# Scattering PEER gates with an accumulating DMA instead of overwriting running sums

## Chip, cores and metric

The kernel runs on one core of a Trainium2 chip. The metric is the device time of one execution in microseconds (us); several executions are timed and their median is compared. TensorE (PE), VectorE (DVE), ScalarE (ACT) and GpSimd (POOL) are the computing engines of the core, and SyncE (SP) only issues DMAs here. POOL issues DMAs too, by an instruction of its own for each (in the profile: DMA_INDIRECT).

## What is computed

One layer of a streaming encoder: a token mixer (two kinds of attention, 8 heads each, one input and one output projection) and then a PEER mixer, in which each token picks single-neuron experts. Only the second half bears on this change. For 512 tokens, 8 PEER heads and 16 experts per head, the reference does this for each block of 128 tokens:

```python
idx = jnp.take_along_axis(cand_i, best_j, axis=-1)       # 8 heads x 16 experts of 16384
g = jax.nn.softmax(best_s, axis=-1)                      # a gate for each
a = gelu(einsum('thkd,td->thk', u_sel, hb))              # u_sel, v_sel: the rows of u and v at idx
out = einsum('thk,thkd->td', g * a, v_sel)
```

The 16 experts of one head are distinct. Two heads of one token can pick the same expert, and then its two gates add up.

## The kernel before, in words

The first 128 tokens are done by gathering: for each of the 128 slots of a token (8 heads by 16) an indirect DMA from POOL (`fetch`, line 824) brings the chosen row of `u`, and later that of `v`, of all 128 tokens into one of three buffers `gr`, 1 MB at a time, and DVE works on it in two halves (`consume`, lines 843 and 846). There are 256 such gathers. `consume(n)` issues the gather of `n + 2`; a buffer comes free when DVE has used the row set that lies in it.

The other 384 tokens (three blocks) are done densely, over all 16384 experts. PE works through a list of items (line 937): A items and D items multiply 128 rows of `u` with the tokens (48 matmuls each, `mm_u`, line 994), R items load activations made earlier, V items multiply by `v` (`mm_v`, line 1016). The list has 108 A items, then 16 D items, then the V and R items. The activation of an A item goes to a DRAM scratch table (`act_out`, line 876). The gates of the dense tokens stand in another DRAM table, `g_scr`, with one number for each expert and token (25 MB), which was zeroed early in the kernel (line 607). D and R items load 192 KB of it (`load_gates`, line 959) and multiply. The first of these loads is issued three items ahead of the first D item.

The table is filled by scatters from POOL: one indirect DMA writes 128 numbers of 4 bytes (one slot of one block of 128 tokens), 8 heads x 16 slots x 3 blocks = 384 of them. A generator, `scatter()` (line 910), hands the work out in steps, and the item loop (line 1049) takes `NSC` steps per A or D item from the third item on (line 1068), with some two of the gathers' halves (`due`, line 858), spread over the four cuts in which the next item's weights are split into a high and a low part (`cut_up`, line 975, with ACT's cast at line 183 and DVE's subtraction at line 184).

Before the change a step of `scatter()` does two things. `total(h, b, i)` (line 911) has DVE compare the expert of one slot with those of all slots of the token up to the same head, and sum the gates where they agree, into `tot`. Then the scatter of the slot of the head before (48 steps earlier) is traced, which writes that sum. An expert that several heads chose is written by each of them in turn, and the last write holds the whole sum. Scatters of one head are declared independent of each other; those of the next head wait until all of the head before have landed. There are 9 x 48 = 432 steps, six per item, so 72 items.

How the order on the engines comes about: inside the item loop PE, DVE, ACT and SP keep the order in which the program is traced (`fixed`, line 1045). POOL is not in that set. Its order is made at build time by a scheduler, which gives POOL the earliest traced instruction among those whose inputs and buffers are ready by its own reckoning; on the chip POOL then works through that order, one after the other.

Of the kernel before, what the change touches and what calls it, by code (L numbers as in the profile page):

```python
# [9 lines left out]
F32 = mybir.dt.float32  # L10
# [5 lines left out]
OP = mybir.AluOpType  # L16
AX = mybir.AxisListType
PSUM = bass.MemoryType.PSUM
DRAM = bass.MemoryType.DRAM

P = 128
# [3 lines left out]
D = 2048  # L25
# [3 lines left out]
TOPK = 16  # L29
PH = 8  # L30
TD0 = 128
TD = T - TD0
NDB = TD // P
# [5 lines left out]
WA = 2.1  # L39
JC = 16  # L40
LEAD = JC // 2 + 1
NSC = 6
AHEAD = 3


class Lanes:
    """Steps of generators, run between pieces of the tensor engine's main stream.

    A generator yields (pieces to wait, next step uses the shared bank)."""

    def __init__(self):
        self.q = {}
# [39 lines left out]
def hymba_peer(ctx: ExitStack, tc: tile.TileContext, xT, w_in, w_fl, b_fg, g_mix, g_q, g_k, g_merge,  # L92
               w_out, g_ffn, w_q, keysT, uT, u, v, out):
    nc = tc.nc

    def pool(name, bufs=1, **kw):
        return tc.tile_pool(name=name, bufs=bufs, **kw)
# [11 lines left out]

    nc.scalar.preload_act_table_set("natural_log_exp_and_others")  # L110

# [1 line left out]
    ident = cst.tile([P, P], F32, name="ident")  # L113
    make_identity(nc, ident)
    identb = cst.tile([P, P], BF16, name="identb")
# [101 lines left out]
    with ExitStack() as fctx:  # L217
        rawx = ExitStack()
        raw = rawx.enter_context(pool("raw", 16))

# [1 line left out]
        KV = [(0, 264), (264, 528)]  # L222
        QR = [(NM, S)]
        raws = [None] * 16

# [1 line left out]
        with ExitStack() as actx:  # L227
            at = actx.enter_context(pool("at", 2))
            qk = actx.enter_context(pool("qk", 1))
# [1 line left out]
            def t2(shape, dtype, name):  # L231
                return at.tile(shape, dtype, name=name, tag="t2", bufs=15)

            # the input, scaled by the gain; each projection is scaled by rstd as it leaves PSUM
            hh, hl = [], []
            flr = raw.tile([P, KD, NH], F32, name="flr", tag="raw")
            flh = raw.tile([P, KD, NH], F32R, name="flh", tag="raw")
# [2 lines left out]
            rstd = raw.tile([P, S], F32, name="rstd", tag="rstd", bufs=1)  # L240
# [3 lines left out]
            for k in range(KD):  # L244
# [25 lines left out]
                a = big.tile([P, S], F32R, name=f"hh{k}", tag="hh")  # L270
                b = big.tile([P, S], F32R, name=f"hl{k}", tag="hl")
# [17 lines left out]
            stx.close()  # L289
            mnx.enter_context(tc.manual_schedule(engines=ordered))  # L290

            # forget gate: cumulative log sigmoid, [head, token]
            fb_ = raw.tile([NH, S], F32, name="fb", tag="raw")
            for i, (lo, hi) in enumerate(KV):
                nc.vector.tensor_tensor(fb_[:, lo:hi], fps[i][:NH, :264], rstd[:NH, lo:hi], op=OP.mult)
# [55 lines left out]
            def pass3(ah, al, bh, bl):  # L351
                return ((ah, bh), (ah, bl), (al, bh))

            # -- stick-breaking head, keys on partitions --
            # (rows, width, [(key block, column offset, first query)])
            units = [(P, 512, [(2, 0, 256), (3, 256, 256)]), (P, 384, [(1, 0, 128)]),
                     (P, 512, [(0, 0, 0)]), (NM, 512, [(4, 0, 0)])]

            def sb_att(c, q, vh, vl):
                zs, sps, tops, sums, wts = {}, {}, {}, {}, {}  # L360
# [25 lines left out]
                    sps[ui] = [(sh, sl, off, t0) for b, off, t0 in blks]  # L386
                    tops[ui] = a

                # sums over the key blocks so far, for the units before them
                def run_on(ui):  # L390
                    a, w = tops[ui], units[ui][1]
                    if ui == 0:
                        w = 256
                        nc.vector.tensor_tensor(a[:, :w], a[:, :w], a[:, w:], op=OP.add)
                    else:
                        pw = sums[ui - 1][2]
                        nc.vector.tensor_tensor(a[:, w - pw:w], a[:, w - pw:w], tops[ui - 1][:, :pw], op=OP.add)
                    rh = t2([P, 512], F32R, f"rh{c}_{ui}")
                    rl = t2([P, 512], F32R, f"rl{c}_{ui}")
                    split(rh[:, :w], rl[:, :w], a[:, :w])  # L400
                    sums[ui] = rh, rl, w
# [74 lines left out]
                lanes.add("misc", v_natural(c, ps, vh, vl), 1, True)  # L476
                lanes.add("att", sb_att(c, q, vh, vl), 1)

            # -- forgetting head, queries on partitions --
            def fox_norm(h, nm, ps, rng, gn, q):  # L480
                off = rng[0][0]
                xs = []
                for i, (lo, hi) in enumerate(rng):
                    w = hi - lo
                    x = t2([P, 512], F32, f"x{nm}{h}{i}")
                    nc.vector.tensor_tensor(x[:, :w], ps[i][:, :w], rstd[:, lo:hi], op=OP.mult)
                    sq = t2([P, 512], F32, f"xs{nm}{h}{i}")
                    nc.scalar.activation(sq[:, :w], x[:, :w], AF.Square)
                    sh = t2([P, 512], F32R, f"xh{nm}{h}{i}")
                    sl = t2([P, 512], F32R, f"xl{nm}{h}{i}")  # L490
                    split(sh[:, :w], sl[:, :w], sq[:, :w])
                    xs.append((x, sh, sl))

                def g():
                    for i, (lo, hi) in enumerate(rng):
                        w = hi - lo
                        x = xs[i][0]
                        pm = pmisc(f"pn{nm}{h}{i}")
                        for n in (1, 2):
                            nc.tensor.matmul(pm[:, :w], nones, xs[i][n][:, :w], start=(n == 1), stop=(n == 2))  # L500
                        y = rsqrt(t2, pm[:, :w], -P, [P, w], f"{nm}{h}{i}")
                        nc.vector.scalar_tensor_tensor(x[:, :w], x[:, :w], gn, y, op0=OP.mult, op1=OP.mult)
                        split(q[nm + "h"][:, lo - off:hi - off], q[nm + "l"][:, lo - off:hi - off], x[:, :w])
                        if i + 1 < len(rng):
                            yield 1, True
                return g()
# [113 lines left out]
            lanes.drain()  # L620
        fcx.close()

# [1 line left out]
        pr = ctx.enter_context(pool("pr", 1, side="right"))  # L624
        hbn = pr.tile([P, D], F32, name="hbn")
        acc = pr.tile([P, D], F32, name="acc")
# [5 lines left out]
        with ExitStack() as mctx:  # L632
# [21 lines left out]
            for _ in merge(1):  # L654
                pass

# [1 line left out]
            ss2 = mt.tile([P, T], F32, name="ss2", bufs=1)  # L658

            def residual(c, ps):  # L660
# [32 lines left out]
            first = [project(w_out[c], mh, ml, [(0, T)], f"wo{c}", hfs=(0,)) for c in range(3)]  # L693
# [6 lines left out]
            ssf = big.tile([P, T], F32, name="ssf", tag="ssf", bufs=1)  # L700
            nc.gpsimd.tensor_copy(ssf, ss2)

# [1 line left out]
        rawx.close()  # L704
        hbx = ExitStack()
        hbd = hbx.enter_context(pool("hbd", 1, side="right"))
# [5 lines left out]
        with ExitStack() as qctx:  # L712
# [89 lines left out]
            for h in range(PH):  # L802
                scs = []
                for p in range(2):
                    c = 2 * h + p
                    key = qp.tile([P, P], F32, name=f"key{c}", tag="key")
# [9 lines left out]

    bigx.close()

# [1 line left out]
    # (table, slot), the up rows of a head before its down rows  # L820
    order = [(x, h * TOPK + i) for h in range(PH) for x in range(2) for i in range(TOPK)]
    rows = {}

# [38 lines left out]
        done[0] = r.stop  # L862
        return [x for n in r for x in (consume(n),) * 2]

# [1 line left out]
    dn = ctx.enter_context(pool("dn", 2))  # L866
    gp = hbx.enter_context(pool("gp", 1, side="right"))
    ef = gp.tile([P, NTB, P], F32, name="ef")
    dst = gp.tile([P, NDB, P], I32, name="dst")
    tot = gp.tile([P, NDB, P], F32, name="tot")  # L870
    def act_out(j, ps, keep=False):
        g = dn.tile([P, TD], F32, name=f"ga{j}", tag="ga")
        nc.scalar.activation(g, ps[:, :TD], AF.Gelu)
# [29 lines left out]
    gt = ctx.enter_context(pool("gt", 3))  # L903
    pq = ctx.enter_context(pool("pq", 2))

    # the gates of the dense tokens, scattered head by head: an expert that several heads chose gets the
    # sum of its gates, written by each of them in turn with the heads so far
    g_flat = g_scr.rearrange("j i (t o) -> (j i t) o", o=1)

    def scatter():  # L910
        def total(h, b, i):
            s, w = h * TOPK + i, (h + 1) * TOPK
            junk = gp.tile([P, P], F32, name=f"junk{h}{b}{i}", tag="junk")
            nc.vector.scalar_tensor_tensor(junk[:, :w], ef[:, b + 1, :w], ef[:, b + 1, s:s + 1],
                                           gts[:, b + 1, :w], op0=OP.is_equal, op1=OP.mult,
                                           accum_out=tot[:, b, s:s + 1])

        slots = [(b, i) for b in range(NDB) for i in range(TOPK)]
        for h in range(PH + 1):
            head = []  # L920
            for b, i in slots:
                if h < PH:
                    total(h, b, i)
                if h > 0:
                    s = (h - 1) * TOPK + i
                    w = nc.gpsimd.indirect_dma_start(  # L926
                        out=g_flat, out_offset=bass.IndirectOffsetOnAxis(ap=dst[:, b, s:s + 1], axis=0),
                        in_=tot[:, b, s:s + 1], in_offset=None)
                    for x in head:
                        tc.declare_no_dep(w.ins, x.ins, reason="the experts of one head differ")  # L930
                    head.append(w)
                yield

    # the tensor engine's order: A(j) makes the activations of experts i*P+j for all i, for later; D(j)
    # makes those of the first chunk, gated at once; R(j) fetches those made before and gates them;
    # V(j, half) adds their values to one half of the output's columns
    items = [("A", j) for j in range(JC + NAP, P)] + [("D", j) for j in range(JC)]
    for c in range(P // JC):
        for x in range(2 * JC):
            half, jj = divmod(x, JC)  # L940
# [7 lines left out]
    def kind(t):  # L948
        return items[t][0] if 0 <= t < len(items) else ""
# [96 lines left out]
    with tc.manual_schedule(engines=fixed):  # L1046
        sc = scatter()
        loaded = 0
        for t in range(len(items) + 1):
# [5 lines left out]
            turn = prev[0] == "V" and prev[1] % JC == JC - 1  # L1055
# [9 lines left out]
            if t == GATES:  # L1065
                gts = gates()
            work = []
            if kind(t) in ("A", "D") and t > GATES:
                work = due(WA) + [sc] * NSC
            elif kind(t) == "V":  # L1070
# [6 lines left out]
            if kind(t) == "V" and items[t][2] == 0 and items[t][1] in (4, 8, 12):  # L1077
                b = len(accd)
# [61 lines left out]
```

## Time and profile before

| | before |
|---|---|
| median of 3 runs | 3520.58 us |
| lowest, highest | 3518.69, 3529.51 us |
| profiled execution, first to last instruction | 3525.9 us |
| mean granted TensorE clock in it | 0.977 of full speed |
| busy: PE, DVE, ACT, POOL | 3398.5, 2402.1, 1296.8, 1096.4 us |

The profile is of one execution. Its time is given as the span from the first to the last instruction, 3525.9 us; no other time of that execution is recorded. The A items lie between 1278 and 2342 us of the span, the D items up to 2477, the V items behind them. Times within the profile are microseconds from the start of the span. A row of the view that groups instructions gives the line, engine, operation, what is written and read, the count, the busy time with the mean of one in ns, and the idle time of the engine just before them with what ended it; "issue" stands for time in which the engine waited for nothing that the profile shows.

### The profile page before, as it was taken

To read this page: it belongs to the slowest core of one execution; us is meant where nothing else is said; L and a number is where in the kernel's file an instruction comes from. 1 tells how busy PE (TensorE), PEld (TensorE's weight loads), DVE (VectorE), ACT (ScalarE), POOL (GpSimd) and SP (SyncE) were. 2 spreads that over 40 slices of the span, in tenths; PEclk is the share of its full clock that TensorE was granted. 3 is DMA by queue.
4 is the path that set the end of the run, shared out by engine and by line. 5 is a ranking of instruction groups with operands and counts; after the bars stand their busy time and mean duration, and the time that the engine had idled before them with its cause. 6 is when DMAs were issued, how large, how long until landed. Compare 5 with 4: busy or idle time off the path is not lost.

```text
span 3525.9 us, 49445 instructions
## 1 busy us (share of the span) xinstructions
PE 3398.5 (96%) x17838; PEld 2999.8 (85%) x17838; DVE 2402.1 (68%) x4939; ACT 1296.8 (37%) x2427; POOL 1096.4 (31%) x916
## 2 busy tenths in 40 slices
PE   8999999999999979789888999999999999999999
PEld 6888899988888779779877899999888888888887
DVE  7555666658449996556656666667777877877775
ACT  5444555444333323222222233333333333333332
POOL 2000000012238637767777611111122122112110
PEclk9999999999999989899888999999999999999999
DMA  3333333323442247667666777888888888888885
GB/s 122 126 105 106 107 106 104 107 87 110 141 132 91 89 147 241 219 204 250 220 205 217 246 287 285 288 292 287 319 305 314 300 313 311 308 310 312 312 306 169
DMA packets 224534, 749.23 MB, mean 212 GB/s; under 512 B 35360, under 2 KB 90784, under 8 KB 190880
## 3 DMA queue, kind: packets, MB, share of 16 engines
q1 hardware_dynamic: 168736, 452.23, 39.4%
q0 software_dynamic: 55552, 293.84, 23.0%
q8 instruction: 140, 2.29, 0.3%
q14 instruction: 106, 0.87, 0.1%
HBM read 690.19 MB, written 55.77 MB: 212 GB/s over the span
## 4 chain that ended last, share of the span: by engine, by line
PE 86%; DVE 8%; issue 3%; DMA 2%; POOL 0%; ACT 0%; SPq 0%; DVEq 0%; POOLq 0%; ACTq 0%
PE pv L1016 30%; PE pa L994 28%; PE pj_wo L212 5%; PE pj_sv L212 3%; PE pj_fv L212 3%; PE pj_sk L212 3%; PE pj_fk L212 3%; PE pj_fq L212 3%; PE pj_fg L212 3%; PE pj_sq L212 2%; DMA gr<-in_u_dram,idx 1%; DVE oh L783 1%; PE pj_wq L212 1%; DVE oh L779 1%; PE po L580 1%
## 5 line engine op out<-in xcount | busy, mean ns | idle before, releaser
L994 PE MATMUL pa<-dh,wl_A 128*128 128x384 f32 x1728 | 599.1, 347 | 46.9 <-DVE wl_A L184 23.3
L994 PE MATMUL pa<-dh,wh_A 128*128 128x384 f32 x1728 | 597.7, 346 | 25.9 <-issue 25.4
L994 PE MATMUL pa<-dl,wh_A 128*128 128x384 f32 x1728 | 598.1, 346 | 22.6 <-issue 22.1
L1016 PE MATMUL pv<-wh_V,pl 128*128 128x512 f32 x1536 | 597.5, 389 | 0.0
L1016 PE MATMUL pv<-wl_V,ph 128*128 128x512 f32 x1536 | 597.5, 389 | 0.0
L1016 PE MATMUL pv<-wh_V,ph 128*128 128x512 f32 x1536 | 597.5, 389 | 0.0
L184 DVE TENSOR_TENSOR wl_A<-wr_u,wh_A 128x512 fp32r<-128x512 f32 x428 | 294.4, 691 | 341.0 <-ACT wh_A L183 218.4
L183 ACT CAST wh_A<-wr_u 128x512 fp32r<-128x512 f32 x432 | 265.5, 620 | 656.2 <-PE pa L994 467.9
L183 ACT CAST wh_V<-wr_v 128x512 fp32r<-128x512 f32 x512 | 317.2, 621 | 507.1 <-PE pv L1016 504.8
L184 DVE TENSOR_TENSOR wl_V<-wr_v,wh_V 128x512 fp32r<-128x512 f32 x510 | 343.2, 689 | 221.7 <-ACT wh_V L183 221.5
L926 POOL DMA_INDIRECT g_scr<-tot,dst x384 | 429.3, 1118 | 149.5 <-issue 84.1
L994 PEld LDWEIGHTS pa<-dh,wl_A 128*128 128x128 f32 x1728 | 335.3, 194 | 61.2 <-issue 35.2
L828 POOL DMA_INDIRECT gr<-in_v_dram,idx x128 | 179.8, 1405 | 631.9 <-DVE acc L846 505.0
L994 PEld LDWEIGHTS pa<-dh,wh_A 128*128 128x128 f32 x1728 | 335.0, 194 | 37.3 <-issue 36.8
L994 PEld LDWEIGHTS pa<-dl,wh_A 128*128 128x128 f32 x1728 | 334.9, 194 | 36.2 <-issue 36.0
L828 POOL DMA_INDIRECT gr<-in_u_dram,idx x128 | 156.6, 1224 | 621.8 <-DVE gr L843 479.7
L1016 PEld LDWEIGHTS pv<-wh_V,ph 128*128 128x128 f32 x1536 | 288.3, 188 | 59.9
L1016 PEld LDWEIGHTS pv<-wl_V,ph 128*128 128x128 f32 x1536 | 288.3, 188 | 59.9
L1016 PEld LDWEIGHTS pv<-wh_V,pl 128*128 128x128 f32 x1536 | 288.3, 188 | 59.8
L843 DVE SCALAR_TENSOR_TENSOR gr<-gr,hbn 128x1024 f32<-128x1024 f32 x256 | 303.0, 1220 | 35.8 <-DMA gr<-in_u_dram,idx 31.1
L846 DVE SCALAR_TENSOR_TENSOR acc<-gr,coef,acc 128x1024 f32<-128x1024 f32 x256 | 318.1, 1284 | 2.0 <-DMA gr<-in_v_dram,idx 1.4
L348 POOL TENSOR_TENSOR osq<-o 128x512 f32<-128x512 f32 x14 | 14.5, 1036 | 525.6 <-ACT o L342 525.6
(388 smaller groups left out, 6197.0 us busy)
## 6 DMA issues: line engine op xcount, KB each, us to landing
wr_u<-in_uT_dram SPq DMA_DIRECT2D x256, 512.0 KB
wr_v<-in_v_dram SPq DMA_DIRECT2D x256, 512.0 KB
g_scr<-zero POOLq DMA_DIRECT2D x16, 1536.0 KB
gg<-g_scr SPq DMA_DIRECT2D x128, 192.0 KB
a_scr<-ga SPq DMA_DIRECT2D x112, 192.0 KB
gb<-a_scr SPq DMA_DIRECT2D x112, 192.0 KB
wr_wo<-in_w_out_dram SPq DMA_DIRECT2D x32, 512.0 KB
wr_wq<-in_w_q_dram SPq DMA_DIRECT2D x32, 512.0 KB
```

The costliest lines, as they stand in the source:

```text
L183: nc.scalar.copy(hi, src)
L184: (lo_eng or nc.vector).tensor_tensor(lo, src, hi.bitcast(F32), op=OP.subtract)
L212: nc.tensor.matmul(ps[i][:, :hi - lo], wt[:, kk, :], ht[k][:, lo:hi], start=(k == 0 and n == 0), stop=(k == KD - 1 and n == 2))
L580: nc.tensor.matmul(po[:, t0:], vv, ww, start=f, stop=True, skip_group_check=not f)
L779: nc.vector.tensor_tensor(oh, abf[:, p].unsqueeze(2).to_broadcast([P, NTB * TOPK, TOPK]), iota16.unsqueeze(1).to_broadcast([P, NTB * TOPK, ...
L783: nc.vector.tensor_tensor(ohv, ohv, i1f[:, :, p, :].unsqueeze(2).to_broadcast([P, NTB, TOPK, TOPK]), op=OP.mult)
L828: nc.gpsimd.indirect_dma_start(out=r, out_offset=None, in_=(u, v)[x], in_offset=bass.IndirectOffsetOnAxis(ap=idx0[:, s:s + 1], axis=0))
L843: nc.vector.scalar_tensor_tensor(r[:, c], r[:, c], 1.0, hbn[:, c], op0=OP.mult, op1=OP.mult, accum_out=dots[:, y, h, i:i + 1])
L846: nc.vector.scalar_tensor_tensor(acc[:, c], r[:, c], coef[:, h, i:i + 1], acc[:, c], op0=OP.mult, op1=OP.add)
L926: w = nc.gpsimd.indirect_dma_start(out=g_flat, out_offset=bass.IndirectOffsetOnAxis(ap=dst[:, b, s:s + 1], axis=0), in_=tot[:, b, s:s + 1] ...
L994: nc.tensor.matmul(ps[:, :TD], wt[:, k % 4, :], ht[k], start=(k == 0 and n == 0), stop=(k == KD - 1 and n == 2))
L1016: nc.tensor.matmul(po["now"][n][b], a[:, bs], w_, start=(jj == 0 and pi == 0), stop=(jj == JC - 1 and pi == 2))
```

## The change

The sums are no longer made. Each of the 384 scatters takes its numbers from the gates themselves (`gts`, the result of `gates()` at line 878) and adds them to what stands in the table (`compute_op=OP.add`). A step is one scatter; four steps are taken per item. The tile `tot` goes, and the loop over slots now has the slot outside and the token block inside. The comments, which the change also strips, are left out here.

```diff
-NSC = 6
+NSC = 4
...
-    tot = gp.tile([P, NDB, P], F32, name="tot")
...
     def scatter():
-        def total(h, b, i):
-            s, w = h * TOPK + i, (h + 1) * TOPK
-            junk = gp.tile([P, P], F32, name=f"junk{h}{b}{i}", tag="junk")
-            nc.vector.scalar_tensor_tensor(junk[:, :w], ef[:, b + 1, :w], ef[:, b + 1, s:s + 1],
-                                           gts[:, b + 1, :w], op0=OP.is_equal, op1=OP.mult,
-                                           accum_out=tot[:, b, s:s + 1])
-
-        slots = [(b, i) for b in range(NDB) for i in range(TOPK)]
-        for h in range(PH + 1):
+        for h in range(PH):
             head = []
-            for b, i in slots:
-                if h < PH:
-                    total(h, b, i)
-                if h > 0:
-                    s = (h - 1) * TOPK + i
+            for i in range(TOPK):
+                for b in range(NDB):
+                    s = h * TOPK + i
                     w = nc.gpsimd.indirect_dma_start(
                         out=g_flat, out_offset=bass.IndirectOffsetOnAxis(ap=dst[:, b, s:s + 1], axis=0),
-                        in_=tot[:, b, s:s + 1], in_offset=None)
+                        in_=gts[:, b + 1, s:s + 1], in_offset=None, compute_op=OP.add)
                     for x in head:
                         tc.declare_no_dep(w.ins, x.ins, reason="the experts of one head differ")
                     head.append(w)
-                yield
+                    yield
```

## Rows read from the trace of the kernel before

**Rows 1.** The page: span, busy time by engine (its part 1), chain by engine (part 4).

```profile
span 3525.9 us, 49445 instructions
...
PE 3398.5 (96%) x17838; PEld 2999.8 (85%) x17838; DVE 2402.1 (68%) x4939; ACT 1296.8 (37%) x2427; POOL 1096.4 (31%) x916
...
PE 86%; DVE 8%; issue 3%; DMA 2%; POOL 0%; ACT 0%; SPq 0%; DVEq 0%; POOLq 0%; ACTq 0%
```

**Rows 2.** Busy time by windows, items A: with scatters, after them, a dense piece.

```profile
core 0: us, PE busy (x) PEld busy (x) DVE busy (x) ACT busy (x) POOL busy (x), PEclk, DMA share, GB/s
1316.00:2036.00 720.00, 638.62 (x3295) 600.02 (x3293) 448.83 (x1273) 195.61 (x345) 514.89 (x457) 0.91 0.70 227
2036.00:2342.00 306.00, 305.46 (x1762) 305.14 (x1761) 193.87 (x280) 105.53 (x186) 49.28 (x41) 1.00 0.81 287
...
2100.00:2200.00 100.00, 100.00 (x579) 100.00 (x578) 63.18 (x75) 34.55 (x60) 17.25 (x14) 1.00 0.80 287
```

**Rows 3.** The same view, four neighbouring stretches while scatters run.

```profile
1573.00:1656.00 83.00, 83.00 (x470) 83.00 (x469) 66.23 (x190) 27.61 (x48) 64.80 (x55) 1.00 0.78 256
1656.00:1700.00 44.00, 29.10 (x97) 20.92 (x96) 13.48 (x41) 6.24 (x11) 30.18 (x30) 0.69 0.47 155
1700.00:1778.00 78.00, 78.00 (x451) 78.00 (x451) 63.73 (x189) 25.86 (x46) 61.41 (x52) 1.00 0.81 261
1778.00:1814.00 36.00, 20.29 (x61) 13.30 (x60) 8.59 (x24) 4.13 (x8) 24.38 (x24) 0.65 0.51 166
```

**Rows 4.** Groups of POOL's instructions, 1316 to 2036 us.

```profile
L926 POOL DMA_INDIRECT g_scr<-tot,dst x384 | 429.3, 1118 | 149.5 <-issue 84.1 <-DVE junk L914 37.3 <-DVE wl_A L184 17.9
L828 POOL DMA_INDIRECT gr<-in_u_dram,idx x41 | 50.4, 1229 | 35.6 <-DVE gr L843 17.3 <-issue 8.8 <-DMA gr<-in_u_dram,idx 8.3
L828 POOL DMA_INDIRECT gr<-in_v_dram,idx x32 | 35.2, 1100 | 15.1 <-issue 7.9 <-DVE acc L846 5.9 <-DVE junk L914 0.6
```

**Rows 5.** POOL in order of time, two gathers with the scatters between them.

```profile
1713.28 0.98 POOL L828 DMA_INDIRECT gr<-in_u_dram,idx  x1 [0.30 <-DMA g_scr<-tot,dst]
1714.57 1.63 POOL L926 DMA_INDIRECT g_scr<-tot,dst  x1 [0.30 <-DVE wl_A L184]
1716.50 1.45 POOL L926 DMA_INDIRECT g_scr<-tot,dst  x1 [0.30 <-DVE gr L843]
1718.26 0.97 POOL L926 DMA_INDIRECT g_scr<-tot,dst  x1 [0.30 <-issue]
1719.53 0.97 POOL L926 DMA_INDIRECT g_scr<-tot,dst  x1 [0.30 <-issue]
1720.81 0.97 POOL L926 DMA_INDIRECT g_scr<-tot,dst  x1 [0.30 <-DVE wl_A L184]
1722.08 1.29 POOL L926 DMA_INDIRECT g_scr<-tot,dst  x1 [0.30 <-DMA g_scr<-tot,dst]
1723.68 1.99 POOL L828 DMA_INDIRECT gr<-in_u_dram,idx  x1 [0.30 <-issue]
```

**Rows 6.** Groups by line, 1316 to 1384.2 us: scatters issued and sums made.

```profile
L926 POOL DMA_INDIRECT g_scr<-tot,dst x38 | 45.9, 1208 | 11.6 <-issue 7.6 <-DVE junk L914 1.5 <-DVE wl_A L184 1.2
...
L914 DVE SCALAR_TENSOR_TENSOR junk<-ef,e 128x16 f32<-128x16 f32 (+1 forms) x49 | 11.4, 232 | 0.9
```

**Rows 7.** DVE's groups of the sums, 1316 to 2036 us.

```profile
L914 DVE SCALAR_TENSOR_TENSOR junk<-ef,e 128x16 f32<-128x16 f32 (+7 forms) x384 | 112.4, 293 | 6.8
...
L914 DVE DVE_READ_ACCUMULATOR junk<-ef,e 128x1 f32 x384 | 31.5, 82 | 0.0
```

**Rows 8.** The scatters' line alone: ns min/median/max, first and last start.

```profile
L926 POOL DMA_INDIRECT g_scr<-tot,dst x384: 963/972/2021, 1318.0 to 2004.7; - x192
L926 POOLq EVENT_SEMAPHORE  x375: 17/17/5282, 1316.3 to 1995.9; - x188
```

**Rows 9.** POOL's groups behind the scatters, 2036 to 2342 us.

```profile
L828 POOL DMA_INDIRECT gr<-in_v_dram,idx x21 | 25.9, 1234 | 132.4 <-DVE acc L846 89.3 <-DVE gr L843 28.7 <-DVE coef L851 14.4
L828 POOL DMA_INDIRECT gr<-in_u_dram,idx x20 | 23.4, 1168 | 135.0 <-DVE gr L843 113.5 <-DVE acc L846 21.5
```

**Rows 10.** The line that loads gates: first and last start.

```profile
L959 SPq DMA_DIRECT2D gg<-g_scr x128: 326/431/1490, 2319.7 to 3421.9; - x128
```

## Prediction

> **What bounds the kernel now.** I read the page first. PE is busy 96% of the span and holds 86% of the chain that ended last [rows 1], so a change on POOL and DVE can only pay where PE is held up. The view by windows shows where. Behind the scatters PE does 579 matmuls in 100 us [rows 2]; at 48 matmuls an item that is 8.29 us an item, the dense pace. While scatters run (1316 to 2036 us) it does 3295, or 68.6 items, in 720 us; at the dense pace these would take 569 us. So **151 us** of the span are lost in this stage, and that is the most the change can gain by speeding it up; the stretch behind it (1762 matmuls in 306 us) loses next to nothing.
>
> Cut finer, the stage falls into two kinds of stretch that alternate [rows 3] (nine thin ones in all; these are two of them). In the dense ones PE is always busy and its clock is granted at 1.00, the level of 2.4 GHz. In the thin ones it does 97 matmuls in 44 us, 61 in 36 us. There the mean grant is 0.69 and 0.65, so part of the time at the lower level of 1.2 GHz, after PE had been left with gaps; that is a consequence. DVE is less busy in the thin stretches than in the dense ones (13.5 of 44 us against 66.2 of 83), so DVE's work is not what is short. The engine that never rests in either is POOL: 64.8 of 83 us, 30.2 of 44 us, and this leaves out 0.30 us in front of nearly every DMA that it issues [rows 5].
>
> That makes POOL's ledger the one to draw up [rows 4]. A scatter costs (429.3 + 84.1) / 384 = 1.337 us of POOL, its "issue" gaps counted. A gather costs (50.4 + 35.2 + 8.8 + 7.9) / 73 = 1.40 us, and there are 73 in 68.6 items, 1.064 an item. At six scatters an item POOL needs 6 x 1.337 + 1.064 x 1.40 = 9.51 us for an item that PE could do in 8.29. **POOL is overloaded while scatters run**, the gathers queue behind scatters on it, and DVE, which works in order, waits for gathers. Behind the scatters POOL waits for DVE instead [rows 9].
>
> **What the change removes.** The 384 sums cost DVE 112.4 + 31.5 = 144 us [rows 7]. DVE is busy 449 of 720 us there [rows 2], under PE's time, so I cost this at nothing on the path; what covers it is DVE's own slack of 271 us. The sums also hold POOL: it waited 37.3 + 17.9 = 55 us for them [rows 4], and these waits go.
>
> **What it adds.** The number of scatters stays 384, with the same 128 offsets and 128 numbers of 4 bytes each. Each must now also read the table. The trace of before has no accumulating DMA. Its bounds are the shortest scatter, 0.963 us, and the longest, 2.021 us [rows 8]; a gain cannot be excluded, since the mean of 1.118 contains scatters stretched beside DVE work that now goes. Of the rows between, the nearest is the gather from `u`, 1.229 us [rows 4], which also issues 128 reads of HBM at offsets. I take it: 0.111 us more for each, 384 x 0.111 = 43 us, so 1.448 us with the gap. I cost the DMA's own time at nothing beside POOL's, as cover it has engines that are 70% busy here against 81% behind [rows 2].
>
> **What it moves.** Four steps an item instead of six reads as a lighter load: 4 x 1.448 + 1.49 = 7.28 us an item, under 8.29. But POOL's order is not the traced one. The trace shows it: by 1384.2 us only 49 sums had been started, while 38 scatters had been issued [rows 6], and the first at 1318.0 [rows 8]; in program order the first scatter stands behind 48 sums. POOL had each scatter moved up some eight items, to just behind its own sum. The sums, which DVE does in order at six an item, were the only thing that spread the scatters. With them gone, a scatter needs `gts` and `dst` alone, which are there before the first of them, and the landing of the head before. So I expect POOL's order to be filled with scatters from the start, at no fewer than six between two gathers, as it takes them now [rows 5], whatever NSC says.
>
> The sum for six: 64 gathers, so 64 / 1.064 = 60.2 items, 499 us at the dense pace. POOL needs 384 x 1.448 = 556, plus 64 x 1.40 = 90. Its other idle time is 720 - 515 - 84 - 17 = 104 us now; 55 of it go with the sums, 49 stay (waits at the seven changes of head, the longest wait on a semaphore is 5.28 us [rows 8], and for gather buffers). The stage takes 556 + 90 + 49 = 695 us, a loss of 196 against 151: **45 us slower**. What is late is what was late before, the gathers, now packed behind scatters for 60 items instead of 69. The span of the profiled execution, 3525.9 us, lies 5.3 us over the median of 3520.58; I take the same difference off again: 3520.6 + 45 = **3566 us**.
>
> The ends of this case: with the scatter at its old 1.118 and no idle time left, 513 + 90 = 603, a loss of 104, 47 us faster; with seven scatters between gathers, 55 gathers and 51.7 items (429 us), 556 + 77 + 104 = 737, a loss of 308, 157 us slower. Its own range is 3474 to 3678 us.
>
> Off the path: scatters end near 2000 us at the latest pace of this case, and the first load of gates is issued at 2319.7 [rows 10], so SP's queue does not wait. The smaller number of steps, and `tot` gone, free room that nothing asks for.
>
> **Rival 1, faster: POOL does keep four an item.** If the order made at build time spaces the scatters (because it reckons an accumulating one dear, or keeps them near their traced place), POOL has 8.29 - 7.28 = 1.01 us spare in each item, the thin stretches do not come up, and the stage runs at the dense pace. The seven waits for a head's landing, at most 7 x 5.28 = 37 us, fall into about 12 us of spare time a head. Gain 114 to 151 us; I take 130: **3391 us**. For it: NSC is lowered, and the removed 55 us. Against it: POOL has moved scatters up before [rows 6]. It decides against my forecast as soon as POOL's order shows five scatters or fewer for each gather.
>
> **Rival 2, much slower: issuing an accumulating scatter is dear.** At the middle between 1.229 and 2.021, 1.625 us, the main case grows by 384 x 0.396 = 152 us (3718); at 2.021 by 304 (3870); I take **3790 us**. It decides from 1.48 us on: then even four an item fill POOL, (8.29 - 1.49) / 4 - 0.22. For it speaks that each number is read as well as written; against it that plain scatter and gather cost POOL nearly the same [rows 4]. The Trainium skill (Collectives: The Full Stack, section on the bandwidth ceiling) says that an adding transfer emits two read descriptors per chunk where a copy emits one; if POOL's time followed the count, three descriptors for two would make 1.118 us into an estimated 1.68. No run here shows it yet.
>
> **Rival 3, no difference:** the thin stretches have another cause that scatters of either kind share, one price per scatter wherever it stands. Then 384 of them lose the same 151 us: **3521 us**. Against it: POOL issues as much per us in the dense stretches (55 instructions in 83 us) as in the thin ones (30 in 44 us), and the dense ones lose nothing [rows 3]. For it: no row names what PE waits for in the thin ones. A last case, small: every accumulating scatter waits for the one before to land. At 5.28 us each, 384 x 6.7 = 2580 us carry the scatters to about 3900 us, past the load of gates at 2320, some 1580 us slower.
>
> **How the numbers follow.** A measurement of this kernel can tell 0.3%, 10.6 us, from no change. Main case 0.50, of which faster 0.10, same 0.06, slower 0.34; rival 1 0.24; rival 2 0.15; rival 3 0.08; the last case 0.03. Faster 0.34, same 0.14, slower 0.52. The range leaves out about a third of rival 1 below, two thirds of rival 2 and the last case above: 3385 to 3760 us. The likeliest case alone has 3474 to 3678.
>
> **What would show it.** Right: in the order of time POOL has six or more scatters between two gathers, the last scatter starts before 2005 us, a mean near 1.23 us, no PE gap behind DVE's sums, and thin stretches as before until the scatters end. Wrong: four scatters a gather and a stage at 579 matmuls per 100 us (rival 1); a mean of 1.5 us or more (rival 2); thin stretches with POOL at rest (rival 3).

## The result, and the profile after

| | before | after |
|---|---|---|
| median of 4 runs each | 3524.47 us | 3842.55 us |
| lowest, highest | 3518.69, 3529.51 us | 3841.15, 3847.18 us |
| ratio to before, 95% interval | | 1.0900, 1.0882 to 1.0917 |
| profiled execution, its time and its span | span 3525.9 us | 3847.18 us, span 3845.5 us |

The changed kernel is **318 us slower**. The forecast was 3566 us with a range of 3385 to 3760, so the direction was right and the size far off.

The page of the changed kernel: span and busy time, to lay beside [rows 1], and its part 3, the DMA queues.

```profile
span 3845.5 us, 48342 instructions
...
PE 3407.7 (89%) x17838; PEld 3036.7 (79%) x17838; DVE 2301.2 (60%) x4171; ACT 1297.9 (34%) x2427; POOL 1301.9 (34%) x916
...
DMA packets 267534, 749.16 MB, mean 195 GB/s; under 512 B 78369, under 2 KB 133793, under 8 KB 233889
...
q0 software_dynamic: 98560, 293.84, 24.4%
```

PE does the same 17838 matmuls in about the same busy time, but its share of the span falls from 96 to 89%: the time that came was idle time of PE. POOL issues the same 916 instructions and is busy 206 us longer. Its DMA queue carries the same bytes in 98560 packets; the page of before has this line for that queue:

```profile
q0 software_dynamic: 55552, 293.84, 23.0%
```

The difference, 43008, is 384 x 112: each of the 384 scatters moves 112 packets more than before.

Where on the way the time was lost, the view by windows of the changed kernel says (columns as in [rows 2]): first the stretch with scatters, then the rest of the A items and the D items.

```profile
1309.00:2130.00 821.00, 428.53 (x2037) 416.73 (x2035) 212.23 (x318) 123.12 (x215) 687.69 (x429) 0.75 0.54 123
2130.00:2663.00 533.00, 532.55 (x3057) 532.55 (x3058) 333.93 (x472) 182.21 (x320) 81.48 (x70) 0.99 0.81 287
```

2037 matmuls are 42.4 items, which at the dense pace of 8.29 us take 352 us; they took 821. So 469 us are lost in this stage where 151 were lost before [rows 2], and the difference, **318 us, is the whole slowdown**. PE stood idle for 392 of the 469 us; the other 77 are matmuls that took longer at a mean granted clock of 0.75, so part of the time at the lower level of 1.2 GHz, after such gaps. The second stretch loses 5 us, next to nothing, as before. POOL's groups in the first one, to lay beside [rows 4]:

```profile
L915 POOL DMA_INDIRECT g_scr<-e,dst x384 | 641.5, 1671 | 117.0 <-issue 115.4 <-DMA g_scr<-e,dst 1.2 <-DVE wl_A L184 0.3
L828 POOL DMA_INDIRECT gr<-in_u_dram,idx x29 | 29.7, 1024 | 8.8 <-issue 8.5 <-DVE wl_A L184 0.3
L828 POOL DMA_INDIRECT gr<-in_v_dram,idx x16 | 17.2, 1077 | 4.9 <-issue 4.9
```

Two things differ. A scatter takes 1.671 us of POOL instead of 1.118, x1.49. And there are 45 gathers for 384 scatters where there were 73 in the stage before. Busy and idle time together are 641.5 + 117.0 + 29.7 + 8.8 + 17.2 + 4.9 = 819.1 us of 821: POOL never rests. The view by line of the scatter (shortest, median and longest in ns, first and last start), to lay beside [rows 8], has every accumulating scatter at 1.557 us or more, where a plain one took 0.963 or more:

```profile
L915 POOL DMA_INDIRECT g_scr<-e,dst x384: 1557/1557/3301, 1309.5 to 2124.1; - x192
L915 POOLq EVENT_SEMAPHORE  x8: 17/17/191, 1305.1 to 2028.0; - x8
```

The second line is the wait of POOL at each of the eight heads, at most 0.19 us: by the time that a head is issued, the one before has landed. POOL in order of time, to lay beside [rows 5]:

```profile
1536.58 1.56 POOL L915 DMA_INDIRECT g_scr<-e,dst  x1 [0.30 <-issue]
1538.44 1.56 POOL L915 DMA_INDIRECT g_scr<-e,dst  x1 [0.30 <-issue]
1540.30 1.01 POOL L828 DMA_INDIRECT gr<-in_u_dram,idx  x1 [0.30 <-issue]
1541.61 1.58 POOL L915 DMA_INDIRECT g_scr<-e,dst  x1 [0.30 <-issue]
1543.50 1.58 POOL L915 DMA_INDIRECT g_scr<-e,dst  x1 [0.30 <-issue]
...
1557.42 1.56 POOL L915 DMA_INDIRECT g_scr<-e,dst  x1 [0.30 <-issue]
1559.29 1.56 POOL L915 DMA_INDIRECT g_scr<-e,dst  x1 [0.30 <-issue]
```

Followed through the whole stage, ten scatters stand between two gathers 29 times, eleven 7 times, fewer only 5 times. The step of four per item is nowhere to be seen in POOL's order. What waits for the gathers is shown by the waits of this stretch (waiter, what it waited for, us in total, times, longest):

```profile
PE pa L983 <- DVE wl_A L184: 368.3, 33, 18.6
DVE gr L843 <- DMA gr<-in_u_dram,idx: 358.2, 23, 19.8
DVE acc L846 <- DMA gr<-in_v_dram,idx: 213.7, 14, 18.8
```

DVE stands 358.2 + 213.7 = 572 us waiting for gathered rows. Behind those waits, in its order, stand the low parts of PE's weights, and PE waits 368 us for them. That is the chain: scatters, late gathers, DVE, PE.

### The profile page after: what moved, and what is told of

The parts are those of the page before. It is cut to its first block, busy times and chain, and to the rows that moved or that the text cites. A ratio compares the mean times of both kernels' runs of the same rounds, so it can differ in the third digit from the quotient of the medians.

```text
span 3845.5 us, 48342 instructions
## 1 busy us (share of the span) xinstructions
PE 3407.7 (89%) x17838; PEld 3036.7 (79%) x17838; DVE 2301.2 (60%) x4171; ACT 1297.9 (34%) x2427; POOL 1301.9 (34%) x916
## 3 DMA queue, kind: packets, MB, share of 16 engines
q0 software_dynamic: 98560, 293.84, 24.4%
## 5 line engine op out<-in xcount | busy, mean ns | idle before, releaser
L983 PE MATMUL pa<-dh,wl_A 128*128 128x384 f32 x1728 | 616.6, 357 | 392.9 <-DVE wl_A L184 392.9
L915 POOL DMA_INDIRECT g_scr<-e,dst x384 | 641.5, 1671 | 117.0 <-issue 115.4
L983 PEld LDWEIGHTS pa<-dh,wl_A 128*128 128x128 f32 x1728 | 348.4, 202 | 404.7 <-DVE wl_A L184 404.7
L983 PE MATMUL pa<-dh,wh_A 128*128 128x384 f32 x1728 | 609.3, 353 | 13.5 <-ACT wh_A L183 13.5
L983 PE MATMUL pa<-dl,wh_A 128*128 128x384 f32 x1728 | 607.4, 351 | 0.0
L843 DVE SCALAR_TENSOR_TENSOR gr<-gr,hbn 128x1024 f32<-128x1024 f32 x256 | 303.0, 1221 | 358.2 <-DMA gr<-in_u_dram,idx 358.2
L846 DVE SCALAR_TENSOR_TENSOR acc<-gr,coef,acc 128x1024 f32<-128x1024 f32 x256 | 318.0, 1284 | 213.7 <-DMA gr<-in_v_dram,idx 213.7
L184 DVE TENSOR_TENSOR wl_A<-wr_u,wh_A 128x512 fp32r<-128x512 f32 x428 | 286.5, 691 | 235.3 <-ACT wh_A L183 230.0
L828 POOL DMA_INDIRECT gr<-in_u_dram,idx x128 | 148.8, 1163 | 675.9 <-DVE gr L843 538.1
L983 PEld LDWEIGHTS pa<-dh,wh_A 128*128 128x128 f32 x1728 | 347.9, 201 | 13.8 <-ACT wh_A L183 13.8
L983 PEld LDWEIGHTS pa<-dl,wh_A 128*128 128x128 f32 x1728 | 346.5, 201 | 0.0
L348 POOL TENSOR_TENSOR osq<-o 128x512 f32<-128x512 f32 x14 | 14.5, 1038 | 525.6 <-ACT o L342 525.6
```

The source lines that it names most:

```text
L184: (lo_eng or nc.vector).tensor_tensor(lo, src, hi.bitcast(F32), op=OP.subtract)
L348: nc.gpsimd.tensor_tensor(sq, r, r, op=OP.mult)
L828: nc.gpsimd.indirect_dma_start(out=r, out_offset=None, in_=(u, v)[x], in_offset=bass.IndirectOffsetOnAxis(ap=idx0[:, s:s + 1], axis=0))
L843: nc.vector.scalar_tensor_tensor(r[:, c], r[:, c], 1.0, hbn[:, c], op0=OP.mult, op1=OP.mult, accum_out=dots[:, y, h, i:i + 1])
L846: nc.vector.scalar_tensor_tensor(acc[:, c], r[:, c], coef[:, h, i:i + 1], acc[:, c], op0=OP.mult, op1=OP.add)
L915: w = nc.gpsimd.indirect_dma_start(out=g_flat, out_offset=bass.IndirectOffsetOnAxis(ap=dst[:, b, s:s + 1], axis=0), in_=gts[:, b + 1, s:s ...
```

## The experiments

The theory: POOL is the engine that sets the pace of the stage, by the ledger of the prediction (scatters per item times their price, plus the gathers), and both entries of the ledger grew, the order (ten scatters a gather) and the price (1.671 us). One rival says price alone: a scatter costs what it costs wherever it stands, and the order does nothing. The other says order alone. Four kernels make a two by two of order and price, and five more test the ledger. The runs came in three sets, each with the kernel before beside it; its median was 3536.68, 3497.53 and 3534.39 us in them, so kernels of different sets are compared by their ratio to it. The sets were taken on three different chips. The kernel before moved by 1.1% between them, the changed kernel by 0.1% between the two on which it ran, so a comparison across sets carries an uncertainty of about 1%.

**Moved up, plain.** The changed kernel, with nothing but the adding taken away.

```diff
-                        in_=gts[:, b + 1, s:s + 1], in_offset=None, compute_op=OP.add)
+                        in_=gts[:, b + 1, s:s + 1], in_offset=None)
```

> The changed kernel with a plain (overwriting) scatter in place of the accumulating one; POOL's order is the same, ten scatters for most gathers. It leaves out the adding up of gates of experts chosen by several heads. If order and price both count (main theory): a scatter takes POOL some 1.0 to 1.12 us and 0.30 us in front, 384 x 1.35 = 518 us, with 45 gathers 575 us for some 42 items (350 us at the dense pace), a loss of 225 us against 151 before: about 3590 to 3600 us. If the price alone made the change slow: as before, 3524 us. If the order alone made it: as the changed kernel, 3843 us.

Measured: 3688.50 us, 1.0437 of before (1.0408 to 1.0466). POOL's order is the one of the changed kernel, ten between gathers 29 times and eleven 7 times, so whatever makes the order does not look at the adding. Groups of POOL in its stage, then the stage by windows:

```profile
L915 POOL DMA_INDIRECT g_scr<-e,dst x383 | 406.1, 1060 | 117.0 <-issue 116.4 <-DMA g_scr<-e,dst 0.6
L828 POOL DMA_INDIRECT gr<-in_u_dram,idx x27 | 29.5, 1091 | 44.9 <-DVE gr L843 37.7 <-issue 7.2
L828 POOL DMA_INDIRECT gr<-in_v_dram,idx x16 | 19.2, 1197 | 32.1 <-DVE acc L846 28.1 <-issue 4.0
```

```profile
1308.40:1957.10 648.70, 418.19 (x1951) 377.02 (x1950) 208.17 (x305) 117.76 (x206) 454.66 (x427) 0.75 0.46 149
```

40.6 items in 648.7 us: a loss of 312. The kernel before and the changed one, also from the first scatter to the last, in this order:

```profile
1318.00:2004.70 686.70, 608.82 (x3125) 570.87 (x3124) 431.08 (x1239) 185.60 (x327) 506.36 (x451) 0.90 0.69 224
```

```profile
1309.50:2124.10 814.60, 428.03 (x2034) 416.23 (x2032) 209.42 (x312) 123.12 (x215) 684.86 (x426) 0.75 0.54 121
```

They lose 147 and 463 us. So there are **165 us for the order alone** (the sums went with it) and **151 more for the price in that order**. Both single-cause theories fall: price alone wanted the loss of before, order alone that of the changed kernel. The time is nevertheless some 80 us above what the ledger had led me to expect (12 us of the difference to 3688 lie in the kernel before of this set). In it POOL spent 37.7 + 28.1 = 66 us waiting for DVE to free a gather's buffer, a time in which the ledger takes it to be busy, and most of PE's gaps are not behind DVE here; the last section returns to both.

**Held, adding and plain.** The changed kernel, with every scatter told to stay behind the gather that is traced before it, so that POOL keeps the traced four per gather (102 gathers, four scatters behind 96 of them, in both traces). The second kernel then also leaves the adding away.

```diff
+    last = [None]
...
-            nc.gpsimd.indirect_dma_start(
+            last[0] = nc.gpsimd.indirect_dma_start(
...
-                    w = nc.gpsimd.indirect_dma_start(
+                    with tc.issue_after(last[0].ins):
+                        w = nc.gpsimd.indirect_dma_start(
```

> The changed kernel with its accumulating scatters, each queued on POOL behind the gather traced before it, so that POOL really has four for each item. If order and price both count: POOL needs 4 x 1.97 + 1.49 = 9.4 us an item against 8.29 at the dense pace, for 96 items a loss of about 104 us against 151 before: 3460 to 3500 us. If the price alone made the change slow: 3843 us, as the changed kernel. If the order alone: the dense pace, 3375 to 3410 us.

> Both undone: plain scatters, each queued behind the gather traced before it, four an item, no sums made (it leaves out the adding up of gates of experts chosen by several heads). If POOL's load bounds the stage of the scatters: 4 x 1.337 + 1.49 = 6.84 us an item, under 8.29, so the loss of 151 us of the kernel before goes but for some tens: 3375 to 3410 us. If the loss before is a price of each scatter wherever it stands: 3524 us.

Measured: adding 3522.78 us, 0.9952 (0.9937 to 0.9967); plain 3412.21 us, 0.9637 (0.9605 to 0.9669). The stages by windows, adding first:

```profile
1308.20:2267.40 959.20, 864.76 (x4717) 853.28 (x4716) 499.16 (x717) 283.92 (x496) 804.79 (x486) 0.95 0.83 242
```

```profile
1308.50:2145.10 836.60, 818.53 (x4625) 808.93 (x4624) 497.74 (x708) 278.24 (x487) 563.39 (x486) 0.99 0.82 275
```

and their scatters in the groups by line, in the same order:

```profile
L917 POOL DMA_INDIRECT g_scr<-e,dst x384 | 676.6, 1762 | 123.6 <-issue 113.4 <-DMA g_scr<-e,dst 9.9 <-ACT wh_A L183 0.3
```

```profile
L917 POOL DMA_INDIRECT g_scr<-e,dst x384 | 445.0, 1159 | 130.4 <-issue 112.8 <-DMA g_scr<-e,dst 17.6
```

The plain one is 2 us over its range, though the kernel before was 12 us slower in this set, and loses 38 us in 96.4 items. The adding one lies above its range: I had taken 1.671 us for a scatter, and spread among more work it took 1.762; 384 x 0.091 = 35 us. At four an item POOL then needs 4.01 x (1.762 + 0.295) + 1.49 = 9.7 us against 8.29, is overloaded again, and loses 144 us. So the price alone costs 111 us even where the order is kept, and the order alone 3688.50 - 3412.21 = 276 us where the price is low. At the high price the order costs 3842.55 - 3522.78 = 320 us (the changed kernel was timed on other chips). There the traces show the chain at both ends; these are the waits of the held adding kernel, to lay beside those of the changed one:

```profile
DVE gr L844 <- DMA gr<-in_u_dram,idx: 135.1, 33, 8.7
DVE acc L847 <- DMA gr<-in_v_dram,idx: 134.5, 32, 10.0
PE pa L985 <- DVE wl_A L184: 93.6, 31, 8.2
```

DVE waits 270 us for gathered rows where it waited 572, and PE 94 us for the low parts where it waited 368.

**The changed kernel again**, unedited, beside the next two.

> The changed kernel itself, on the chip of these runs, so that every comparison stands on the same footing. Every theory: 1.085 to 1.095 of the kernel before, as on the first chip (1.09).

Measured: 3845.36 us, 1.1002 (1.0980 to 1.1025). Its own time is that of the first chip; the ratio is above what was expected because the kernel before took 3497.53 us here.

**Six an item without sums.** The held plain kernel, with `NSC = 6`. It asks whether DVE's sums had been what the kernel before lost its time by.

> Plain scatters of the single gates (the adding up of gates of an expert that several heads chose is left out), held at six an item behind the item's gathers, and no sums on DVE. The ledger theory: POOL needs 6 x (1.10 + 0.30) + 1.49 = 9.9 us an item against 8.29, for 64 items, so a loss of about 100 us in the stage beside the 30 that the other held kernels keep; by the number of gathers it is 384 / 6 = 64 items in some 635 us. Against the held four an item (3412 us on its chip, 0.9637 of before) some 90 to 130 us more, so 3500 to 3545 us, 0.985 to 1.00 of before, although the sums are gone. The rival theory that DVE's sums caused the loss of the kernel before: without sums it stays at 0.96 to 0.97 of before.

Measured: 3501.32 us, 1.0010 of before (1.0001 to 1.0020). Without a single sum on DVE, and with the same 67 gathers among the scatters, the time is that of the kernel before. The sums cost nothing in time, and the stage still loses 116 us without them (3190 matmuls in 666.8 us). What PE's gaps end with is another question, for the last section.

**Fewer steps an item, sums kept.** The kernel before with 4.25 steps an item, and with five. Nothing is left out of the computation.

```diff
-                work = due(WA) + [sc] * NSC
+                work = due(WA) + [sc] * (t * 17 // 4 - (t - 1) * 17 // 4)
```

> The kernel before, with its sums and plain scatters, but 4.25 steps an item on average in place of six (432 steps in 102 items); it computes the whole reference. If POOL's load bounds the stage: 4.25 x 1.337 + 1.49 = 7.2 us an item, under 8.29: 3375 to 3420 us, faster than both kernels. If the loss is a price of each scatter or of the sums on DVE: 3524 us.

```diff
-NSC = 6
+NSC = 5
```

> The kernel before with five steps of the scatter an item in place of six, nothing left out. The ledger theory: 5 x 1.40 + 1.49 = 8.5 us an item, just over 8.29, for 86 items, so 18 us of loss beside the 30 that the kernel with 4.25 an item keeps: 0.965 to 0.98 of before. The rival theory, a price for each scatter wherever it stands: no difference from before (1.00), and the 0.9624 of 4.25 an item has another cause.

Measured: at 4.25 steps 3403.63 us, 0.9624 (0.9602 to 0.9647); at five 3430.83 us, 0.9820 (0.9796 to 0.9845), a little over the range. POOL's order follows the sums in each: four or five scatters between gathers at 4.25 (90 times of 91), five at five (68 times of 77), as it was six at six (58 times of 64). The stages by windows, 4.25 first:

```profile
1318.50:2095.30 776.80, 762.72 (x4333) 754.34 (x4332) 553.04 (x1419) 258.86 (x455) 568.43 (x480) 0.99 0.82 276
```

```profile
1316.70:2013.20 696.50, 669.39 (x3763) 664.26 (x3761) 492.05 (x1340) 225.51 (x396) 538.10 (x464) 0.98 0.80 265
```

The same 384 scatters at nearly the same price (means of 1.194, 1.148 and 1.118 us) lose 28 us at 4.25 an item, 47 at five and 147 at six. It is their density, not their number, that costs. At 4.25 this is the kernel that **beats both**, by 3.8% and without an accumulating DMA.

**Holding, with the sums.** The kernel before and the one with 4.25 steps, with the scatters held behind the gather traced before them, as above.

> The kernel before, its sums and its six steps an item kept, with each scatter held behind the gather that is traced before it, so that POOL cannot move scatters up. Nothing is left out. In the kernel before PE's gaps are mostly put down to issue, in the kernels with held scatters to late gathers. If those gaps are only another face of the overloaded POOL, the time stays within 1% of before (0.99 to 1.00), as without the sums. If they are a cost of their own that the moved-up order brings, they go and the time falls by up to their 70 us, to 0.98 of before.

> The kernel with sums and 4.25 steps an item, with its scatters held behind the gather traced before them; nothing is left out. The ledger has spare time on POOL in either order, so by it nothing changes: 0.958 to 0.968 of before. If holding costs something (a scatter that is ready has to wait for a gather that waits for DVE), it shows here as more, up to 0.975.

Measured: at six 3541.34 us, 1.0016 (0.9996 to 1.0036); at 4.25 3421.66 us, 0.9679 (0.9636 to 0.9722). At six the first scatter moves from 1318.0 to 1375.9 us, so holding does what it says, and the time does not change. The gaps that the profile puts to "issue" did not go, so the second branch of that expectation found nothing to test. At 4.25 the result is at the edge of "no change": POOL waited 55.8 + 44.7 us ahead of gathers where it had waited 25.9 + 34.4 without holding, but the intervals of the two kernels overlap, and the price of holding stays unsettled. Where the sums pace the scatters already, it gains nothing.

**The ledger over ten kernels.** Each row is the stage from the first scatter to the last. Gathers are those of POOL in it; scatters per item are 384 / gathers x 1.064; POOL's need is that times the scatter's mean and its "issue" gap, plus 1.49 us; the pace is the length of the stage by its items.

| kernel | gathers | scatter + gap, us | POOL's need, us an item | pace, us an item |
|---|---|---|---|---|
| held, plain, four | 102 | 1.453 | 7.3 | 8.7 |
| sums at 4.25 | 96 | 1.424 | 7.6 | 8.6 |
| held, sums at 4.25 | 97 | 1.495 | 7.8 | 8.9 |
| sums at 5 | 81 | 1.317 | 8.1 | 8.9 |
| before, sums at 6 | 67 | 1.337 | 9.6 | 10.5 |
| held, sums at 6 | 68 | 1.429 | 10.1 | 10.7 |
| held, adding, four | 102 | 2.057 | 9.7 | 9.8 |
| held, plain, six | 67 | 1.434 | 10.2 | 10.0 |
| moved up, plain | 43 | 1.367 | 14.5 | 16.0 |
| after | 43 | 1.971 | 20.2 | 19.2 |

Below PE's 8.29 the pace stays near it, above it the pace is POOL's need within some 10%. One ledger holds for plain and adding scatters, with sums and without, held and moved up. The table alone does not show the cause: the program fixes the gathers of an item, so wherever POOL never rests, its need and the pace agree by themselves. That the load is the cause is shown by the edits, which changed the load and with it the time.

## Why the prediction was wrong, step by step

- **What bounds the kernel** (POOL overloaded, gathers late, DVE behind them, PE behind DVE): right for the changed kernel, where the waits name that chain outright. For the kernel before, POOL's load is shown, and the ten kernels follow the ledger, but the chain behind it is not shown. Its waits from 1316 to 2036 us, the lines below, have PE mostly at "issue" and hardly behind DVE, and DVE little behind gathers. And POOL does rest there, against my reading: in the last stretch of [rows 3] it is busy for 24.38 us, which with 24 gaps of 0.30 us makes 31.6 of 36.

```profile
PE pa L994 <- issue: 70.3, 101, 3.0
PE pa L994 <- DVE wl_A L184: 9.3, 3, 5.5
DVE gr L843 <- DMA gr<-in_u_dram,idx: 31.1, 9, 8.0
```

- **The sums cost nothing**: right; without them, at the same six an item, 1.0010 of before. The 55 us that POOL waited for them did go, and bought nothing, since POOL filled them with more scatters.
- **The 0.111 us more for an accumulating scatter** (taken from the gather from `u`, 1.229 us, as the nearest row): wrong, and the first step that failed. It measured 0.553 us more, 1.671 us. A gather also reads at 128 offsets, but it is not the same work. The sentence on the Trainium skill (Collectives: The Full Stack, section on the bandwidth ceiling), two read descriptors per chunk for an adding transfer (stated there for the reduce step of a collective), gave an estimate of 1.68 us, and the trace agrees with that figure. Some of that is luck: against a plain scatter in the same order (1.063 us) the factor is 1.57 and not 1.5. The trace doesn't agree with the count: the packets of a scatter grew by 112, and not by half. By an estimate from the software queue that is from about 33 to about 145: it moved 22886 packets in the stage of before and 61881 in that of the changed kernel, of which I take off 140 for each gather. The figure may therefore be right for another reason, and no run here tells which.
- **"No fewer than six between two gathers"** with six in the sum: the lower bound held, the value did not, and this is the second step that failed. It was ten. I had seen that only the sums spaced the scatters, and concluded that without them POOL's order would be filled; then I took the spacing that the sums had made as the spacing without them. Seven was my upper end, without a row behind it. With no sum to wait for, nothing in the trace of before bounded the number.
- **The sum itself**: its form was good. With the measured values, 43 gathers are 43 / 1.064 = 40.4 items, 335 us at the dense pace; POOL needs 384 x 1.971 + 43 x 1.40 = 817 us. The loss is 482 us, 331 more than 151, and the trace has 318. Two inputs were wrong, and in this sum they add: 384 x 0.523 = 201 us for the price, 21 x (8.29 / 1.064 - 1.40) = 134 us for the 21 gathers fewer, less the 49 us of idle time that did not stay. With the 45 of the forecast that makes the 331.
- **Rival 1** (POOL keeps four an item, 3391 us) fell, since the order was not kept. Where it is made to keep it, the adding kernel is at 0.9952 of before, 0.5% faster, and not at 0.963, because the price holds there too.
- **Rival 2** (dear issue, 3790 us) named one of the two causes and was the nearest. Its mean of 1.5 us or more and its 1.625 us middle were passed. It was priced with six a gather, and at 1.671 us that alone would have been near 3736; I gave it 0.15, and no case at all to its meeting with a denser order.
- **Rival 3** (one price per scatter wherever it stands) fell with the kernels at 4.25 and five. **The serialised case** fell: 0.19 us at most is waited at a head, and within one the next scatter follows after 0.30 us.
- **Off the path**: scatters ended at 2124 us instead of 2005 at the latest, still well ahead of the first load of gates, which moved to 2640.6 us.

The range failed because it took the two uncertain inputs one at a time: the dear price with six a gather, or seven a gather with the likely price. Ten a gather and the dear price came together.

## What to carry to other kernels

A dependence that is removed may have been the only thing that paced an engine whose order is made by readiness; then a lower number of steps in the program may say nothing (four in the program were ten on POOL here), and the question is what spaces the work now. Draw up the ledger of the issuing engine per item of the critical engine (instructions by their price, gaps counted) before trading one kind of DMA for another: 128 separate adds are not 128 separate writes. And when such a ledger is over the item's time, try the plain remedy first, here fewer steps per item, which gave 3.8% with one edited line.

## What was not expected of the hardware

An accumulating indirect DMA of 128 numbers held POOL for 1.552 to 1.557 us at the least where the plain one took 0.963 to 0.968, in every kernel, and moved 112 more packets. The mean rises with the work around it: 1.671 us adding and 1.063 plain in the thin stage, 1.762 and 1.159 in the denser one.

PE's gaps come in two kinds. In both kernels with accumulating scatters, in the plain one without sums at six an item and in the one with sums at five, they end with DVE, which waited for gathers. In the kernel before, in the moved-up plain one and in the held one with sums at six, most of them are put to "issue". The view in order of time of the moved-up plain kernel shows what they look like, PE alone:

```profile
1411.10 0.48 PE L983 MATMUL pa<-dl,wh_A 128*128 128x384 f32 x1 [1.41 <-issue]
1413.20 0.48 PE L983 MATMUL pa<-dh,wl_A 128*128 128x384 f32 x1 [1.63 <-issue]
1415.30 0.48 PE L983 MATMUL pa<-dh,wh_A 128*128 128x384 f32 x1 [1.62 <-issue]
1418.80 0.48 PE L983 MATMUL pa<-dl,wh_A 128*128 128x384 f32 x1 [3.01 <-issue]
```

In these rows one matmul starts every 2.10 or 3.50 us, multiples of 0.70 us, while POOL issues plain scatters without a pause; the waits of the stage put 209 us of PE's idle time to such gaps, and 17 us in the kernel with held plain scatters at four an item. I take the 66 us that POOL waited for DVE in that kernel to be their consequence (DVE works at the pace of PE's items), but this is argued and not shown. What PE waits for in them no view shows, and how much of the 276 us of the order at the low price comes by way of late gathers stays open with it.

Nor do the runs settle what brings these gaps. At six an item, held, the first of these rows is without the sums and the second with them:

```profile
PE pa L985 <- DVE wl_A L184: 81.7, 22, 11.8
```

```profile
PE pa L996 <- issue: 87.6, 116, 2.3
```

The time against before was the same both ways. But the two ran on different chips. On the chip of the first, where the kernel before took 3497.53 us, none of the three profiled kernels has such a gap, the one with sums at five among them. In the other profiles every kernel with plain scatters has some (14 to 209 us), and the two with accumulating scatters have none. So it may be the chip and not the sums that decides; a kernel with plain scatters profiled on more than one chip would tell, and none was.
